# A batched fp32 matrix product on one core: engine programs written out by hand, a loop on TensorE, and loads with longer source runs

## The chip, the cores and the metric

The kernel runs on one core of a Trainium2 chip. A core has TensorE (PE in the profile, with its weight loads as PEld), VectorE (DVE), ScalarE (ACT), GpSimd (POOL) and SyncE (SP), which here issues every data transfer, and 16 DMA engines, which carry them out. The metric is the device time of one execution in microseconds; a figure for a kernel is the median of its runs.

## The reference

```python
def setup_inputs():
    batch, m, k, n = 16, 512, 768, 1024
    return {
        "x": np.random.randn(batch, k, m).astype(np.float32),
        "y": np.random.randn(batch, k, n).astype(np.float32),
    }

def reference(x: np.ndarray, y: np.ndarray) -> np.ndarray:
    return np.einsum('bkm,bkn->bmn', x, y).astype(np.float32)
```

For each of 16 batches a 768 x 512 matrix, transposed, is multiplied by a 768 x 1024 matrix. Inputs and output are fp32 in DRAM: 75.5 MB are read and 33.55 MB written.

## The kernel before

**Tiling.** K = 768 is split as 128 partitions times 6, with k = 6p + ko, so partition p of an x tile holds six consecutive rows of x, which are 12 KB in a row in DRAM, and partition p of a y tile holds 24 KB in a row. The output's 512 rows are split as 128 partitions times 4, m = 4p + mo, so that an output partition is 16 KB in a row. `x_w` (line 71) picks, for each `mo`, the 128 columns of x that belong to it.

**Stages of a batch b.** SP loads x (line 59) and y (line 62) into fp32 tiles `xs` and `ys`. DVE casts x to bf16 (line 67) and y in two halves of three ko each (line 70). PE runs 48 matmuls of 128 x 128 by 128 x 512 (line 83): for each `mo` of 4, for each half `nt` of N, six ko that add up in PSUM. After each `mo` ACT copies 1,024 columns of `ps` into `o_sb` (line 88). SP stores the whole 2 MB of `o_sb` (line 52), `LAG` = 4 batches later: in SP's order the store of batch b-4 follows the loads of batch b (lines 63 and 64), and the last four stores stand at the end (lines 89 and 90).

**Buffers.** Pools give two buffers each of `xs`, `ys`, `x_sb` and `y_sb`, five of `o_sb`, and four of `ps` with two PSUM banks each.

**Order and waits.** The program is written for one pass in order, `tc.manual_schedule()` keeps this order on each engine, and the tile framework derives the semaphore waits from the buffers. So the load of x of batch b waits for the cast of x of batch b-2 (which frees `xs`), and the load of y of batch b for the casts of y of batch b-2. The cast of x of batch b waits for the matmuls of batch b-2, which read the same `x_sb`. The engines' programs are unrolled: PE has 768 weight loads and 768 matmuls in a row.

**Last batch.** For b = 15 `halves` is 2: y is loaded in two transfers of three ko, and PE takes the first three ko of all output columns, then the other three, so that it can begin on half of y.

Of the kernel before, what the change touches and what calls it, by code (L numbers as in the profile page):

```python
# [1 line left out]

_os.environ.setdefault("NEURON_RT_ULTRASERVER_MODE", "4")

# [1 line left out]

# [4 lines left out]


@with_exitstack
def kernel(
    ctx: ExitStack,
    tc: tile.TileContext,
    x: bass.AP,
    y: bass.AP,
    out: bass.AP,
):  # L20
    nc = tc.nc
    P = 128
    FP32 = mybir.dt.float32
    BF16 = mybir.dt.bfloat16

    B, K, M = x.shape
    _, _, N = y.shape
    KT = K // P
    MT = M // P
    NF = 512  # L30
    NT = N // NF

    x_v = x.rearrange("b (p ko) m -> b p ko m", ko=KT)
    y_v = y.rearrange("b (p ko) n -> b p ko n", ko=KT)
    o_v = out.rearrange("b (p mo) n -> b p mo n", mo=MT)

    xs_pool = ctx.enter_context(tc.tile_pool(name="xs_pool", bufs=2))
    ys_pool = ctx.enter_context(tc.tile_pool(name="ys_pool", bufs=2))  # L40
    x_pool = ctx.enter_context(tc.tile_pool(name="x_pool", bufs=2))
    y_pool = ctx.enter_context(tc.tile_pool(name="y_pool", bufs=2))
    o_pool = ctx.enter_context(tc.tile_pool(name="o_pool", bufs=5))
    psum = ctx.enter_context(tc.tile_pool(name="psum", bufs=4, space=bass.MemoryType.PSUM))
    LAG = 4
    KH = KT // 2
    o_tiles = {}

    def store(b):
        o_sb = o_tiles.pop(b)  # L50

        nc.sync.dma_start(o_v[b], o_sb[:])

    with tc.manual_schedule():
        for b in range(B):
            xs = xs_pool.tile([P, KT, M], FP32, name="xs")
            ys = ys_pool.tile([P, KT, N], FP32, name="ys")
            halves = 2 if b == B - 1 else 1
            nc.sync.dma_start(xs[:], x_v[b])  # L59
            for h in range(halves):  # L60
                ks = slice(h * KT // halves, (h + 1) * KT // halves)
                nc.sync.dma_start(ys[:, ks], y_v[b, :, ks])
            if b >= LAG:
                store(b - LAG)
            x_sb = x_pool.tile([P, KT, M], BF16, name="x_sb")
            y_sb = y_pool.tile([P, KT, N], BF16, name="y_sb")
            nc.vector.tensor_copy(x_sb[:], xs[:])  # L67
            for h in range(2):
                ks = slice(h * KH, (h + 1) * KH)
                nc.vector.tensor_copy(y_sb[:, ks], ys[:, ks])  # L70
            x_w = x_sb[:].rearrange("p k (j mo) -> p k mo j", mo=MT)
            o_sb = o_pool.tile([P, MT, N], FP32, name="o_sb")
            o_tiles[b] = o_sb
            ps = {}


            for h in range(halves):
                for mo in range(MT):
                    if h == 0:
                        ps[mo] = psum.tile([P, NT, NF], FP32, name="ps")  # L80
                    for nt in range(NT):
                        for kt in range(h * KT // halves, (h + 1) * KT // halves):
                            nc.tensor.matmul(  # L83
                                ps[mo][:, nt], x_w[:, kt, mo],
                                y_sb[:, kt, nt * NF:(nt + 1) * NF],
                                start=(kt == 0), stop=(kt == KT - 1))
                    if h == halves - 1:
                        nc.scalar.copy(o_sb[:, mo].rearrange("p (t f) -> p t f", f=NF), ps[mo][:])  # L88
        for b in sorted(o_tiles):
            store(b)  # L90


# [1 line left out]
_INS = ['x', 'y']  # L94
_OUTS = [((16, 512, 1024), 'float32')]


# [23 lines left out]
```

## Time and profile before

| | us |
|---|---|
| median of 10 runs (261.58 to 262.20) | 262.01 |
| the profiled execution | 261.74 |
| its span, from the first instruction to the last | 260.0 |

| in the span | busy us | instructions |
|---|---|---|
| PE matmuls (line 83) | 186.3 | 768 |
| PE weight loads | 88.5 | 768 |
| DVE casts (lines 67 and 70) | 83.1 | 48 |
| ACT copies (line 88) | 64.9 | 64 |

PE, PEld, DVE and ACT work beside each other, so their busy times don't add up to the span. The profile cuts the span into 40 slices of 6.5 us. The DMA row of the slices gives, in tenths, the mean busy share of the 16 DMA engines; the row below it gives what they moved. The queue rows give the number of packets, the megabytes and the share of 16 engines' span: q1 is SP's queue of data transfers, and q8 and q14 carry instructions to the engines. Each transfer here makes 128 data packets, one for each partition, eight on each DMA engine, and 16 completion marks of 4 bytes, one from each engine. In the chain of waits each piece is followed back to what released it. In timeline lines the columns are start, duration, engine, line, operation and tiles, and in brackets the idle time before and what ended it.

The profile shows SP issuing the transfers in 0.3 to 0.4 us each. The median from issue to landing is 29.7 us for x, 28.1 us for y and 32.6 us for a store.

### The profile page before, as it was taken

To read this page: it belongs to the slowest core of one execution; us is meant where nothing else is said; L and a number is where in the kernel's file an instruction comes from. 1 tells how busy PE (TensorE), PEld (TensorE's weight loads), DVE (VectorE), ACT (ScalarE), POOL (GpSimd) and SP (SyncE) were. 2 spreads that over 40 slices of the span, in tenths; PEclk is the share of its full clock that TensorE was granted. 3 is DMA by queue.
4 is the path that set the end of the run, shared out by engine and by line. 5 is a ranking of instruction groups with operands and counts; after the bars stand their busy time and mean duration, and the time that the engine had idled before them with its cause. 6 is when DMAs were issued, how large, how long until landed. Compare 5 with 4: busy or idle time off the path is not lost.

```text
span 260.0 us, 1815 instructions
## 1 busy us (share of the span) xinstructions
PE 186.3 (72%) x768; PEld 88.5 (34%) x768; DVE 83.1 (32%) x48; ACT 66.2 (25%) x65; POOL 0.2 (0%) x4
## 2 busy tenths in 40 slices
PE   0049999898939949698594987939679394899600
PEld 0014555453513414243151442514334152355200
DVE  0271734525222252322524214252132522252000
ACT  1003343333321313314032140412314033131600
POOL 0000000000000000000000000000000000000000
PEclk9999999999986988979799797998999899799975
DMA  6999999999999999999999999999999999999995
GB/s 272 431 424 427 446 418 439 435 372 429 436 432 424 436 422 444 422 433 422 437 435 427 437 420 437 434 422 441 425 430 433 413 442 422 426 432 429 434 429 232
DMA packets 7065, 109.18 MB, mean 420 GB/s; under 512 B 784, under 2 KB 784, under 8 KB 784
## 3 DMA queue, kind: packets, MB, share of 16 engines
q1 hardware_dynamic: 7056, 109.06, 98.5%
q8 instruction: 6, 0.10, 0.1%
q14 instruction: 3, 0.02, 0.0%
HBM read 75.50 MB, written 33.55 MB: 419 GB/s over the span
## 4 chain that ended last, share of the span: by engine, by line
DMA 74%; DVE 11%; PE 8%; ACT 0%; issue 0%; SPq 0%; DVEq 0%
DMA ys<-in_y_dram 74%; DVE y_sb L70 11%; PE ps L83 8%; ACT o_sb L88 0%; SPq L59 0%; DVEq L70 0%
## 5 line engine op out<-in xcount | busy, mean ns | idle before, releaser
L83 PE MATMUL ps<-y_sb,x_sb 128*128 128x512 bf16 x768 | 186.3, 404 | 58.1 <-DVE y_sb L70 58.1
L83 PEld LDWEIGHTS <-x_sb 128*128 128x128 bf16 x768 | 88.5, 117 | 155.5 <-issue 39.6
L88 ACT COPY o_sb<-ps 128x1024 f32<-128x1024 f32 x64 | 64.9, 1014 | 178.6 <-PE ps L83 178.6
L70 DVE CAST y_sb<-ys 128x3072 bf16<-128x3072 f32 x32 | 54.9, 1756 | 87.7 <-DMA ys<-in_y_dram 87.7
L67 DVE CAST x_sb<-xs 128x3072 bf16<-128x3072 f32 x16 | 28.2, 1760 | 65.8 <-DMA xs<-in_x_dram 65.5
L88 ACT ACT_TABLE_LOAD x1 | 1.3, 1283 | 0.7 <-PEq L105 0.7
L105 POOL MEMSET const-bfloat16-1.0<- 128x1 bf16 x1 | 0.1, 101 | 0.0
L105 POOL MEMSET const-uint8-127<- 128x1 uint8 x1 | 0.1, 101 | 0.0
L105 POOL MEMSET const-float32-0.0<- 128x1 f32 x1 | 0.1, 98 | 0.2 <-issue 0.2
L105 POOL MEMSET const-float32-1.0<- 128x1 f32 x1 | 0.1, 98 | 0.0
## 6 DMA issues: line engine op xcount, KB each, us to landing
ys<-in_y_dram SPq DMA_DIRECT2D x15, 3072.0 KB, 28.1
out_dram<-o_sb SPq DMA_DIRECT2D x16, 2048.0 KB, 32.6
xs<-in_x_dram SPq DMA_DIRECT2D x16, 1536.0 KB, 29.7
ys<-in_y_dram SPq DMA_DIRECT2D x2, 1536.0 KB, 26.1
```

The lines of the kernel that those rows point to most:

```text
L67: nc.vector.tensor_copy(x_sb[:], xs[:])
L70: nc.vector.tensor_copy(y_sb[:, ks], ys[:, ks])
L83: nc.tensor.matmul(ps[mo][:, nt], x_w[:, kt, mo], y_sb[:, kt, nt * NF:(nt + 1) * NF], start=(kt == 0), stop=(kt == KT - 1))
L88: nc.scalar.copy(o_sb[:, mo].rearrange("p (t f) -> p t f", f=NF), ps[mo][:])
L105: nc = _bacc.Bacc("TRN2", target_bir_lowering=False, num_devices=1)
```

## The change

Instead of one program from which the framework derives the waits, each engine's program is written out with its own semaphores, inside a `tile_critical` region:

- **Semaphores.** `sx`, `sy` and `so` count finished transfers by buffer, `ready` counts casts that PE has not yet used, `room` counts free PSUM buffers, `groups` counts finished groups of 24 matmuls (two per batch), and `outs` counts finished output batches at the end.
- **PE** runs a loop of eight passes, each with two batches (`batch(0)`, `batch(1)`), so that the buffers' addresses are fixed. It takes credits: it waits for `ready` or `room` and subtracts what it took. [...] PE's list shrinks from 1,536 weight loads and matmuls to a body of 192 matmuls with their weight loads and a branch.
- **PSUM** is two buffers of four banks, one for each group (two `mo`), and ACT copies 2,048 columns at once: 32 copies in place of 64.
- **SP** loads x and y of batch b once the first group of batch b-2 is done (`groups` at 2(b-2)+1). The store of batch b waits for all groups of batch b+1, and for the last two batches for `outs`.
- **Wide loads.** `wide_dma` builds the first load of x and of y as before. From batch 1 on it makes the source access pattern of 32 rows of 48 KB for x (four partitions' worth) and of 64 rows of 48 KB for y (two partitions' worth); the destination stays 128 partitions of 12 KB or 24 KB.
- **Last batch.** y of batch 15 is loaded in one transfer, and PE goes through it like any other batch.
- At the end SP waits for each of the five `so`.

DVE's casts and their number, the matmuls, the bytes moved, the number of buffers in SBUF, and the order of the transfers on SP are the same, except for the split of the last y.

The launch code and the imports (`copy`, and `OrderedEngineSet`, which names the engines of a loop) are left out here.

```diff
@@ -36,58 +38,121 @@
     y_v = y.rearrange("b (p ko) n -> b p ko n", ko=KT)
     o_v = out.rearrange("b (p mo) n -> b p mo n", mo=MT)
 
-    xs_pool = ctx.enter_context(tc.tile_pool(name="xs_pool", bufs=2))
-    ys_pool = ctx.enter_context(tc.tile_pool(name="ys_pool", bufs=2))
-    x_pool = ctx.enter_context(tc.tile_pool(name="x_pool", bufs=2))
-    y_pool = ctx.enter_context(tc.tile_pool(name="y_pool", bufs=2))
-    o_pool = ctx.enter_context(tc.tile_pool(name="o_pool", bufs=5))
-    psum = ctx.enter_context(tc.tile_pool(name="psum", bufs=4, space=bass.MemoryType.PSUM))
     LAG = 4
+    NO = 5
     KH = KT // 2
-    o_tiles = {}
+
+    ctx.enter_context(tc.tile_critical())
+    ec = ctx.enter_context
+    xs = [ec(nc.sbuf_tensor(f"xs{i}", [P, KT, M], FP32)) for i in range(2)]
+    ys = [ec(nc.sbuf_tensor(f"ys{i}", [P, KT, N], FP32)) for i in range(2)]
+    xb = [ec(nc.sbuf_tensor(f"xb{i}", [P, KT, M], BF16)) for i in range(2)]
+    yb = [ec(nc.sbuf_tensor(f"yb{i}", [P, KT, N], BF16)) for i in range(2)]
+    ob = [ec(nc.sbuf_tensor(f"ob{i}", [P, MT, N], FP32)) for i in range(NO)]
+
+    HB = MT // 2
+    ps = [ec(nc.psum_tensor(f"ps{i}", [P, HB, NT, NF], FP32)) for i in range(2)]
+    sx = [ec(nc.semaphore(f"sx{i}")) for i in range(2)]
+    sy = [ec(nc.semaphore(f"sy{i}")) for i in range(2)]
+    so = [ec(nc.semaphore(f"so{i}")) for i in range(NO)]
+    ready = ec(nc.semaphore("ready"))
+    room = ec(nc.semaphore("room"))
+    groups = ec(nc.semaphore("groups"))
+    outs = ec(nc.semaphore("outs"))
+
+
+    made = {}
+
+    def wide_dma(key, dst, src, dram_rows, load):
+
+
+        if key not in made:
+            made[key] = nc.sync.dma_start(dst, src)
+            return made[key]
+        pat = mybir.BassSymbolicTensorAccessPattern
+        widen = lambda a: a.rearrange("(q r) k m -> q (r k m)", r=dram_rows)
+        plain = lambda a: a.rearrange("p k m -> p (k m)")
+        s, d = (widen(src), plain(dst)) if load else (plain(src), widen(dst))
+        return nc.sync.add_instruction(_copy.replace(
+            made[key].ins, name=nc.get_next_instruction_name(),
+            ins=(pat(ap=s.ap, dtype=s.dtype, bass_ap=s, is_dma=False),),
+            outs=(pat(ap=d.ap, dtype=d.dtype, bass_ap=d, is_dma=False),),
+            sync_info=None, ant_dge_precooked=False))
+
 
     def store(b):
-        o_sb = o_tiles.pop(b)
-
-        nc.sync.dma_start(o_v[b], o_sb[:])
-
-    with tc.manual_schedule():
-        for b in range(B):
-            xs = xs_pool.tile([P, KT, M], FP32, name="xs")
-            ys = ys_pool.tile([P, KT, N], FP32, name="ys")
-            halves = 2 if b == B - 1 else 1
-            nc.sync.dma_start(xs[:], x_v[b])
-            for h in range(halves):
-                ks = slice(h * KT // halves, (h + 1) * KT // halves)
-                nc.sync.dma_start(ys[:, ks], y_v[b, :, ks])
-            if b >= LAG:
-                store(b - LAG)
-            x_sb = x_pool.tile([P, KT, M], BF16, name="x_sb")
-            y_sb = y_pool.tile([P, KT, N], BF16, name="y_sb")
-            nc.vector.tensor_copy(x_sb[:], xs[:])
-            for h in range(2):
-                ks = slice(h * KH, (h + 1) * KH)
-                nc.vector.tensor_copy(y_sb[:, ks], ys[:, ks])
-            x_w = x_sb[:].rearrange("p k (j mo) -> p k mo j", mo=MT)
-            o_sb = o_pool.tile([P, MT, N], FP32, name="o_sb")
-            o_tiles[b] = o_sb
-            ps = {}
 
 
-            for h in range(halves):
-                for mo in range(MT):
-                    if h == 0:
-                        ps[mo] = psum.tile([P, NT, NF], FP32, name="ps")
-                    for nt in range(NT):
-                        for kt in range(h * KT // halves, (h + 1) * KT // halves):
-                            nc.tensor.matmul(
-                                ps[mo][:, nt], x_w[:, kt, mo],
-                                y_sb[:, kt, nt * NF:(nt + 1) * NF],
-                                start=(kt == 0), stop=(kt == KT - 1))
-                    if h == halves - 1:
-                        nc.scalar.copy(o_sb[:, mo].rearrange("p (t f) -> p t f", f=NF), ps[mo][:])
-        for b in sorted(o_tiles):
-            store(b)
+        if b < B - 2:
+            nc.sync.wait_ge(groups, 2 * (b + 2))
+        else:
+            nc.sync.wait_ge(outs, b - (B - 3))
+        nc.sync.dma_start(o_v[b], ob[b % NO][:]).then_inc(so[b % NO], 16)
+
+    for b in range(B):
+        i = b % 2
+        if b >= 2:
+
+            nc.sync.wait_ge(groups, 2 * (b - 2) + 1)
+        wide_dma("x", xs[i][:], x_v[b], 4, True).then_inc(sx[i], 16)
+        wide_dma("y", ys[i][:], y_v[b], 2, True).then_inc(sy[i], 16)
+        if b >= LAG:
+            store(b - LAG)
+    for b in range(B - LAG, B):
+        store(b)
+
+
+    for b in range(B):
+        i = b % 2
+        n = 16 * (b // 2 + 1)
+        if b >= 2:
+            nc.vector.wait_ge(groups, 2 * (b - 1))
+        nc.vector.wait_ge(sx[i], n)
+        nc.vector.tensor_copy(xb[i][:], xs[i][:]).then_inc(ready, 1)
+        nc.vector.wait_ge(sy[i], n)
+        for h in range(2):
+            ks = slice(h * KH, (h + 1) * KH)
+            nc.vector.tensor_copy(yb[i][:, ks], ys[i][:, ks]).then_inc(ready, 1)
+
+
+    def batch(i):
+        x_w = xb[i][:].rearrange("p k (j mo) -> p k mo j", mo=MT)
+        nc.tensor.wait_ge(ready, 2).then_inc(ready, -2)
+        for g in range(2):
+            nc.tensor.wait_ge(room, 1).then_inc(room, -1)
+            for m in range(HB):
+                for nt in range(NT):
+                    for kt in range(KT):
+                        if g == 0 and m == 0 and nt == 0 and kt == KH:
+                            nc.tensor.wait_ge(ready, 1).then_inc(ready, -1)
+                        mm = nc.tensor.matmul(
+                            ps[g][:, m, nt], x_w[:, kt, g * HB + m],
+                            yb[i][:, kt, nt * NF:(nt + 1) * NF],
+                            start=(kt == 0), stop=(kt == KT - 1))
+            mm.then_inc(groups, 1)
+
+    pe = nc.tensor.engine
+    with nc.Fori(0, B // 2, engines=OrderedEngineSet([pe]), head_slot={pe: 0}):
+        batch(0)
+        batch(1)
+
+
+    nc.scalar.nop().then_inc(room, 2)
+    for b in range(B):
+        if b >= NO:
+            nc.scalar.wait_ge(so[b % NO], 16 * (b // NO))
+        for g in range(2):
+            nc.scalar.wait_ge(groups, 2 * b + g + 1)
+            cp = nc.scalar.copy(ob[b % NO][:, g * HB:(g + 1) * HB].rearrange("p m (t f) -> p m t f", f=NF),
+                                ps[g][:])
+            if b < B - 1:
+                cp.then_inc(room, 1)
+        if b == B - 2:
+            nc.scalar.drain().then_inc(outs, 1)
+    cp.then_inc(outs, 1)
+
+    for i in range(NO):
+        nc.sync.wait_ge(so[i], 16 * len(range(i, B, NO)))
```

## The prediction

> **What bounds the kernel now.** I read the page first: busy shares, the slices, the DMA queues, the chain. Then the chain in order of time, the timeline of the first 25 us, the stages, and last the packet records behind the DMA rows.
>
> The page, queues and slices:
>
> ```profile
> span 260.0 us, 1815 instructions
> ...
> DMA  6999999999999999999999999999999999999995
> GB/s 272 431 424 427 446 418 439 435 372 429 436 432 424 436 422 444 422 433 422 437 435 427 437 420 437 434 422 441 425 430 433 413 442 422 426 432 429 434 429 232
> DMA packets 7065, 109.18 MB, mean 420 GB/s; under 512 B 784, under 2 KB 784, under 8 KB 784
> ...
> q1 hardware_dynamic: 7056, 109.06, 98.5%
> q8 instruction: 6, 0.10, 0.1%
> q14 instruction: 3, 0.02, 0.0%
> ```
>
> The 16 DMA engines are busy from slice 1 to the last one. No engine program has that: PE 72%, DVE 32%, ACT 25%. So work taken off PE, DVE or ACT is worth nothing by itself; only what starts the transfers sooner, makes them shorter, or evens them out over the 16 engines moves the end.
>
> The stages (span, PE, PEld, DVE, ACT, POOL, clock, DMA share, GB/s) say the same:
>
> ```profile
> 15.00:40.00 25.00, 23.29 (x98) 11.40 (x98) 13.32 (x8) 7.27 (x8) 0.00 (x0) 1.00 1.01 433
> ...
> 160.00:200.00 40.00, 31.91 (x137) 15.45 (x136) 12.13 (x7) 11.15 (x11) 0.00 (x0) 0.94 1.01 432
> ...
> 240.00:260.00 20.00, 4.42 (x21) 2.09 (x19) 0.00 (x0) 4.05 (x4) 0.00 (x0) 0.74 0.86 366
> ```
>
> A batch moves 6.8 MB, so at 430 GB/s it takes 15.85 us, and in the chain the loads of y follow each other by 31.7 us per two batches. The end of the chain:
>
> ```profile
> 190.93 28.08 DMA ys<-in_y_dram
> ...
> 219.10 3.44 DVE y_sb L70 x2
> 222.54 0.04 issue
> 222.59 21.84 PE ps L83 x93
> 244.43 0.02 issue
> 244.45 1.01 ACT o_sb L88
> ```
>
> It stops at 245.5 with the last copy, but the span ends at 260.0. The last store is issued at 245.5 and lands 13.6 us later, though its eight 16 KB packets per engine need only 8 x 0.61 = 4.9 us: it stands behind store 14. The tail is transfers too, with a good 8 us to spare for PE and ACT.
>
> The packet records refine it. Typical packets took 460 ns (12,288 B), 611 ns (16,384 B) and 912 ns (24,576 B); all of q1 together makes 255.9 us per engine. There is next to no idle left. What is left is unevenness: the 16 completion marks of one transfer lie 1.11 us apart for the first x and 2.80 us apart for the last store. Each 16 KB fetch on q8 (at 37.5, 68.2, 115.4, 153.3, 195.3 and 237.3 us, 0.9 to 1.1 us each) makes one engine late: at 115.36 a fetch took 1.01 us, and a y packet at 116.36 took 1.41 instead of 0.91. That is about 1.5 us for the engine hit, and nothing brings an engine back. After one fetch one mark lags, after six, six lag. The end is set by the latest engine.
>
> [...] the PE instructions on record before the six fetches number 175, 435, 707, 949, 1201 and 1473, about 256 apart. No loop is in this trace. [...] Here 12,288 B more cost 452 ns more, 27.2 GB/s per engine[...] Here successive 12,288 B packets of one engine start 457 ns apart, 5 ns over their 452 ns[...]
>
> **Part by part.** The sum is against the profiled execution: 261.74 us, which is its span of 260.0 and 1.74 around it. It lies 0.27 below the median of 262.01; I carry that difference over.
>
> *PE loop.* PE's 1,538 unrolled instructions become one loop of 192 matmuls, run eight times. With their weight loads that is 384 and a few control instructions: [...] the six fetches go. What is late next is the natural spread of 1.1 us, so the gain is 2.80 - 1.11 = 1.7. Three 8 KB fetches of other engines (191, 197 and 223 us, 0.31 us each) may stay; I take -1.5, between -1.7 and, with every pass fetching, +1.3 (rival B). A back edge that stalls PE is covered: PE waits 3 to 4 us for y_sb before each batch from batch 4 on ("3.30 <-DVE y_sb" at 220.9), and the edge is reached while earlier matmuls still run. Without that cover each of seven edges would cost what its stall has beyond those 3 us, first in PE's time, and in the end's only past the 8 us of the tail.
>
> *Load waits.* Before, x of batch b+2 is issued after the cast of x of batch b, y after the casts of y. Now both, and the store behind them in SP's order, wait for the first group (24 matmuls) of batch b. In steady state nothing comes of it: the group ends some 9 us after y of batch b has landed, and three more transfers and a store (4.9 + 3.7 + 7.3 + 4.9 = 20.8 us) are queued then. At the start it bites. Before, the issues were:
>
> ```profile
> 1.64 0.42 SPq L59 DMA_DIRECT2D xs<-in_x_dram  x1
> 2.10 0.84 SPq L62 DMA_DIRECT2D ys<-in_y_dram  x1
> ...
> 9.19 0.33 SPq L59 DMA_DIRECT2D xs<-in_x_dram  x1
> ...
> 18.12 0.33 SPq L62 DMA_DIRECT2D ys<-in_y_dram  x1
> ...
> 24.30 1.02 ACT L88 COPY o_sb<-ps 128x1024 f32<-128x1024 f32 x1 [1.58 <-PE ps L83]
> ```
>
> The second copy, at 24.30, shows when 24 matmuls are done: 24.2. That is the issue of x of batch 2, instead of 9.19. From issue to first packet the first transfer took 1.0 us (0.73 to 1.74), so the new data starts at 25.2, spread by 1.1. The first four loads end between 24.55 and 25.63. The engines thus stand still for 0.65 us if they restart in the order in which they ran dry, and the last one for up to 1.3 us if not. I take +0.8 (0.5 to 1.3). Batch 3's loads come at 34.5 + 1.0 against a queue that then lasts until 36.3, batch 4's at about 45 + 1 against 48: no second gap.
>
> *Wide loads.* From batch 1 on, x is read as 32 rows of 48 KB instead of 128 of 12 KB, y as 64 of 48 KB instead of 128 of 24 KB; the SBUF side keeps its rows. Per engine and batch 6 + 4 = 10 reads fewer; 15 batches x 10 x 5 ns = 0.75 us if the 5 ns sit on the read side, 0 if on the write side. No row here tells: -0.4 (-0.75 to 0).
>
> *Tail.* y of batch 15 is no longer split, PSUM goes out in 32 copies of 2,048 instead of 64 of 1,024. y lands by about 234, its first cast takes 1.76, 48 matmuls 10.5 to 12.5, the last copy about 2 x 1.0, issue and start 1.4: store 15 is ready at 249 to 251.5; the first engines finish store 14 at 251.5. Zero, and what is lost at worst hits engines that are ahead. Stores 12 to 14 wait for a later batch's groups or for ACT, and come over 7 us before their turn.
>
> *Start and end.* A further hop between SP and the other engines at the start, and five completion waits at the end. The whole start barrier shows before as one wait of 0.7 us (ACT on PE's sequencer): I take a part of that for the hop and the end together, +0.2 (0 to 0.6). The added drain and the credits sit on ACT and PE, inside their idle time.
>
> Sum: -1.5 + 0.8 - 0.4 + 0.2 = -0.9; 260.8 for the profiled execution, 261.1 as a median.
>
> **Rivals.**
>
> *B, the loop is fetched anew.* For it: [...] nothing in the trace excludes it. [...] At 1.5 us for the engine hit, 16 put one on every engine, and the end is 1.5 + 1.1 against 2.8 before: a gain of only 0.2. Above 16, some engine is hit twice, 3.0 + 1.1: 1.3 later than before. With the other terms (+0.6) that is 261.74 + 1.9, about 263.9 as a median. It ends slower from about 16 fetches on; at 6 to 8 it is +0.6.
>
> *C, the wide loads change which engine writes which partitions.* [...] The place is every load from batch 1 on. [...] It decides as soon as packets of loads take longer than 460 or 912 ns by over 1%. For it: nothing but the missing row. [...]
>
> *D, gain and gap cancel.* The fetches stop, but the restart at 25 us takes the whole 1.3 and the read side gives nothing, with 0.6 for start and end: 262.0 to 262.5. For it: the sum's terms are all of one size.
>
> **How the numbers follow.** The forecast A has 0.55, B 0.22, C 0.08, D 0.15. A measurement of this kernel tells about 0.2% (0.5 us) from no change. A alone lies between 260.1 (all terms at their best: -1.7 + 0.5 - 0.75 = -1.95 from the median) and 262.0; 0.3 for the spread of the runs goes below it. Faster: A 0.41, B 0.03, D 0.02, in all 0.46. Same: A 0.13, B 0.06, D 0.06: 0.25. Slower: A 0.01, B 0.13, C 0.08, D 0.07: 0.29. The range reaches up to B's price and leaves C out: 259.8 to 263.9.
>
> **What would show it.** In the changed kernel's page: q8 with no more than two packets (A) or 16 and more (B); the marks of the last store within about 1.3 us; a dent in the GB/s row at 25 us; load packets at their old time per byte (against C); the last copy before 249. Wrong would be an end that moves without the q8 row moving, or a gap beyond the first 30 us.

## The result: 1.9% slower, and the profile after

The changed kernel takes 266.93 us (median of 9 runs, 265.86 to 268.0) against 261.95 us before (30 runs): a ratio of 1.0193, interval 1.0182 to 1.0204. The prediction had 261.1 us and a range up to 263.9. The profiled execution took 265.57 us, with a span of 263.6; it is the fastest of its kind, so its profile shows a loss of 3.8 us (265.57 against 261.74), where the medians differ by 5.0.

The page of the changed kernel, span, DMA slices and queues:

```profile
span 263.6 us, 1831 instructions
...
DMA  7996999997989999899999989999899999989995
GB/s 258 434 466 276 418 418 418 380 455 301 495 370 447 470 420 442 378 470 415 470 395 415 485 368 442 470 418 452 383 457 420 465 395 418 475 372 433 433 420 234
...
q1 hardware_dynamic: 4512, 109.05, 97.6%
q8 instruction: 1, 0.02, 0.0%
q14 instruction: 1, 0.01, 0.0%
```

The engines still carry the time: 97.6% of the span on q1. The instruction fetches did go, from six on q8 to one. Packets fell from 7,056 to 4,512, since a 48 KB source row now counts as one. The dent is in the fourth slice (19.8 to 26.4 us): DMA at 6 tenths, 276 GB/s.

The stage (span, PE, PEld, DVE, ACT, POOL, clock, DMA share, GB/s) from 24 to 28 us in the kernel before:

```profile
24.00:28.00 4.00, 4.00 (x21) 2.05 (x19) 2.34 (x2) 2.03 (x2) 0.00 (x0) 1.00 1.02 436
```

and that stage with two later ones in the changed kernel:

```profile
24.00:28.00 4.00, 4.00 (x21) 2.09 (x19) 0.95 (x1) 1.87 (x1) 0.00 (x0) 1.00 0.61 209
...
34.00:38.00 4.00, 4.00 (x20) 2.14 (x19) 0.00 (x0) 1.87 (x1) 0.00 (x0) 1.00 0.91 393
...
46.00:50.00 4.00, 4.00 (x21) 2.06 (x19) 0.00 (x0) 1.87 (x1) 0.00 (x0) 1.00 0.97 406
```

SP's timeline of the changed kernel, its fifth to tenth transfer:

```profile
25.33 0.47 SPq L70 DMA_DIRECT2D xs<-in_x_dram  x1
25.85 0.59 SPq L70 DMA_DIRECT2D ys<-in_y_dram  x1
35.69 0.47 SPq L70 DMA_DIRECT2D xs<-in_x_dram  x1
36.21 0.59 SPq L70 DMA_DIRECT2D ys<-in_y_dram  x1
47.58 0.47 SPq L70 DMA_DIRECT2D xs<-in_x_dram  x1
48.09 0.59 SPq L70 DMA_DIRECT2D ys<-in_y_dram  x1
```

Before, the load of x of batch 2 was issued at 9.19 us; here at 25.33, while the first DMA engine had finished all four first loads at 24.81 and the last at 27.02. (Such times are those of the completion marks of a transfer: it has landed when the last of its 16 marks is there. VectorE's cast of the first x, for one, starts at 8.78 us, after marks from 6.51 to 8.75.) The loads of batches 2, 3 and 4 are 10 to 12 us apart, which is TensorE's time for one batch. TensorE's own timeline says why: it is dense there.

```profile
23.63 17.21 PE L128 MATMUL ps<-yb,xb 128*128 128x512 bf16 x79
```

The end of the chain in order of time:

```profile
241.78 10.72 PE ps L128 x45
252.50 0.02 issue
252.52 1.86 ACT ob L146
```

As before it stops at the last copy, now 254.4 us. Store 14 ends on the first engine at 255.33 and on the last at 257.61; store 15 follows at once and ends on the last at 262.43. So no time was lost at the tail itself. Nearly all of it lies ahead of batch 5: y of that batch has landed at 79.92 us instead of 76.31, and from then on a batch takes 15.83 us, against 15.85 before.

### The profile page after: what moved, and what is told of

Its sections match the earlier page's. It is cut to its first block, busy times and chain, and to the rows that moved or that the text cites. A ratio compares the mean times of both kernels' runs of the same rounds, so it can differ in the third digit from the quotient of the medians.

```text
span 263.6 us, 1831 instructions
## 1 busy us (share of the span) xinstructions
PE 186.3 (71%) x768; PEld 86.7 (33%) x768; DVE 83.0 (31%) x48; ACT 61.1 (23%) x33; POOL 0.2 (0%) x4
## 3 DMA queue, kind: packets, MB, share of 16 engines
q1 hardware_dynamic: 4512, 109.05, 97.6%
## 5 line engine op out<-in xcount | busy, mean ns | idle before, releaser
L128 PE MATMUL ps<-yb,xb 128*128 128x512 bf16 x768 | 186.3, 403 | 66.2 <-PEq L122 59.2
L128 PEld LDWEIGHTS ps<-yb,xb 128*128 128x128 bf16 x768 | 86.7, 116 | 165.3 <-issue 99.4
L146 ACT COPY ob<-ps 128x2048 f32<-128x2048 f32 x32 | 59.8, 1869 | 192.3 <-PE ps L128 192.3
L115 DVE CAST yb<-ys 128x3072 bf16<-128x3072 f32 x32 | 54.9, 1756 | 88.8 <-DMA ys<-in_y_dram 88.8
L111 DVE CAST xb<-xs 128x3072 bf16<-128x3072 f32 x16 | 28.2, 1760 | 69.8 <-DMA xs<-in_x_dram 69.8
```

The lines of the kernel that those rows point to most:

```text
L111: nc.vector.tensor_copy(xb[i][:], xs[i][:]).then_inc(ready, 1)
L115: nc.vector.tensor_copy(yb[i][:, ks], ys[i][:, ks]).then_inc(ready, 1)
L128: mm = nc.tensor.matmul(ps[g][:, m, nt], x_w[:, kt, g * HB + m], yb[i][:, kt, nt * NF:(nt + 1) * NF], start=(kt == 0), stop=(kt == KT - 1))
L146: cp = nc.scalar.copy(ob[b % NO][:, g * HB:(g + 1) * HB].rearrange("p m (t f) -> p m t f", f=NF), ps[g][:])
```

## The experiments

Each kernel is the changed one with the edit shown; the ratio is to the kernel before, whose median was 262.1 to 262.2 us in these comparisons. Two theories led: **L**, the late issue of loads costs the time, and **W**, the wide reads do.

### Early waits

The load of x of batch b waits for the cast of x of batch b-2, and y for the casts of y, as before the change.

```diff
+    cast = ec(nc.semaphore("cast"))
-            nc.sync.wait_ge(groups, 2 * (b - 2) + 1)
+            nc.sync.wait_ge(cast, 2 * (b - 2) + 1)
         wide_dma("x", xs[i][:], x_v[b], 4, True).then_inc(sx[i], 16)
+        if b >= 2:
+            nc.sync.wait_ge(cast, 2 * (b - 2) + 2)
...
         nc.vector.tensor_copy(xb[i][:], xs[i][:]).then_inc(ready, 1)
+        nc.vector.drain().then_inc(cast, 1)
...
             nc.vector.tensor_copy(yb[i][:, ks], ys[i][:, ks]).then_inc(ready, 1)
+        nc.vector.drain().then_inc(cast, 1)
```

> The changed kernel (266.93 us), but the loads of batch b wait, as in the kernel before, for the casts of batch b-2 (a new semaphore, raised by VectorE after the x cast and after the y casts) and not for TensorE's first group. Theory L (the late issue makes the gap at 25 us, and each late restart brings slow packets after it): x of batch 2 is issued near 10 us, the slices show no dent at 25 us, and the time falls by 2 to 3 us, to 264 to 265. Theory W (the wide reads are slow when the queue is short): slow packets stay at 38 and 50 us and the time stays above 265.5. Theory S (the start is slower by itself, 1.4 us at the landing of the first x): the first x still lands at 8.7 us rather than 7.4.

Measured: 262.86 us, ratio 1.0031 (1.0021 to 1.0041). That is 4.07 us less than the changed kernel, more than L itself had expected. The first issues in SP's timeline, and the first two of the same stages:

```profile
10.76 0.47 SPq L71 DMA_DIRECT2D xs<-in_x_dram  x1
19.73 0.47 SPq L71 DMA_DIRECT2D ys<-in_y_dram  x1
21.75 0.47 SPq L71 DMA_DIRECT2D xs<-in_x_dram  x1
30.72 0.47 SPq L71 DMA_DIRECT2D ys<-in_y_dram  x1
```

```profile
24.00:28.00 4.00, 4.00 (x20) 2.13 (x19) 0.78 (x1) 1.87 (x1) 0.00 (x0) 1.00 0.92 393
...
34.00:38.00 4.00, 4.00 (x21) 2.05 (x20) 0.00 (x0) 1.53 (x1) 0.00 (x0) 1.00 1.04 442
```

The stage at 24 us goes from 0.61 to 0.92 busy. TensorE does the same work in it (4.00 us busy in both), which is why only the DMA column tells the two apart. The share counts a packet where it starts, so with 48 KB packets a full stage can read under or over 1 (0.92 and 1.04 above).

The packet records add the size. Idle time is meant per engine, and "slow" is the time by which packets took over 0.05 us more than is usual for their size, also per engine:

```
                         changed kernel   early waits
idle, 24 to 28 us             2.05            0
idle, 36 to 40 us             0.21            0
slow, 24 to 30 us             0.58            0
slow, 34 to 42 us             0.37            0
slow, 48 to 54 us             0.47            0
slow, 54 to 62 us             1.13            0.56
```

The differences add up to 4.2 us per engine. The idle time is half of it. The other half is slow packets: up to 2.7 us instead of 1.82 after the restart and at the start of the next two loads, which were issued only 2 to 3 us ahead of their turn, and up to 2.97 us in y of batch 4 (2.61 with early waits). The sum is close to the 4.07 us between the medians, but it doesn't prove them, for these two executions differ by only 2.34 us (265.57 and 263.23). With early waits the engines lose time later on: store 15 is issued at 252.20 us, after the first engine has finished store 14 (251.45), and they stand still there for 1.1 us each. The latest engine doesn't wait, but it is further behind the others (the marks of store 14 are 3.72 us apart, 2.28 in the changed kernel), and it sets the end. So the table shows where the time goes, and its split is no more than rough. L holds, W falls here already; S holds as well, since the first x still lands at 8.90 us.

### Plain loads, with late and with early waits

```diff
-        if key not in made:
+        if True:
```

> The changed kernel with every load built as the first one is (128 rows on both sides); the late waits stay. Theory L: the gap at 25 us stays and the time is within 1 us of the changed kernel, 266 to 268. Theory W: the slow packets after 25 us go and the time falls to 263 to 265. If the wide reads save what the packets suggest (1,824 against 4 x 457 ns), the steady batch takes 0.02 us more than with them.

> Both edits at once: early waits and plain loads, so that the PE loop, the two PSUM buffers and the hand-written waits remain. Theory L: as the run with early waits alone, within 0.5 us. Theory W: better than that one by 1 us and more. If the saved instruction fetches are worth 1.5 us at the end, as the prediction had it, this run is below the kernel before: 260.5 to 261.5; if the start is slower by itself, it is 262 to 263.

Measured: plain loads with late waits 266.49 us (1.0177, 1.0146 to 1.0208, so not told apart from the changed kernel); with early waits 263.04 us (1.0031, 1.0020 to 1.0043) against 262.86 with wide loads. The idle stretch at 25 us (2.2 us) and the slow packets after it are there with plain loads too. So the wide reads are not to blame, and they bring about 0.2 us at most: most packets of 49,152 bytes took 1,815 or 1,829 ns, against 4 x 457 = 1,828 ns or 2 x 909 = 1,818. The last theory of this expectation, a saving of 1.5 us from the fetches, fell.

### The loop written out again, with early waits

```diff
-    with nc.Fori(0, B // 2, engines=OrderedEngineSet([pe]), head_slot={pe: 0}):
+    for _ in range(B // 2):
         batch(0)
         batch(1)
```

> Early waits and wide loads, but TensorE's loop written out as eight passes in a row[...]. If fetches matter as the prediction had it: six or more 16 KB fetches come back, the completion marks of the last store spread over 2.5 us and more, and the time is 1 to 1.7 us above the run with early waits alone. If the spread of the marks comes from the start and not from fetches: within 0.5 us of it.

The page has the six fetches back:

```profile
q8 instruction: 6, 0.10, 0.1%
```

Measured: 262.76 us, 1.0021 (1.0013 to 1.0029), the same as the loop's 262.86. The marks of store 14 lie 3.68 us apart here and 3.72 us with the loop. In the loop kernel one engine falls behind at once: there is a jump to the placed head (`head_slot`) at 1.14 us and one fetch of 931 ns at 4.27 us, in the middle of the first load. The marks of the first x are 2.35 us apart with it and 1.08 without, and the first x has landed at 8.90 us and 7.55: most of what S saw is this fetch.

It delays TensorE's start too. All eight kernels with the placed head have such a fetch (at 4.1 to 4.6 us), and their first y has landed at 16.03 to 16.49 us; in the four without it (this one and the next three) it has at 14.71 to 15.04. VectorE's cast of it, in the changed kernel and in the first of the next three:

```profile
16.08 3.43 DVE L115 CAST yb<-ys 128x3072 bf16<-128x3072 f32 x2 [5.54 <-DMA ys<-in_y_dram]
```

```profile
14.74 3.43 DVE L119 CAST yb<-ys 128x3072 bf16<-128x3072 f32 x2 [5.53 <-DMA ys<-in_y_dram]
```

### Loop kernels with the fetch elsewhere, and with none

Three edits on top of the early waits. The first drops the placed head, and the other two keep that and add one edit each:

```diff
-    with nc.Fori(0, B // 2, engines=OrderedEngineSet([pe]), head_slot={pe: 0}):
+    with nc.Fori(0, B // 2, engines=OrderedEngineSet([pe])):
```

> The run with early waits[...]. Theory F (the jump to a fresh block brings a 16 KB fetch at 4.3 us that makes one engine 1.3 us late in the first x load, so one fetch costs the end as much as six did): no 16 KB fetch at 4 us, the marks of the first x within 1.2 us instead of 2.35, and, [...] 261.6 to 262.2. If the body now [...] is fetched anew in each pass: ten or more 16 KB fetches and 263 to 264.5. If the 2.35 us have another cause: unchanged, 262.6 to 263.1.

Measured: 262.86 us, 1.0025 (1.0014 to 1.0036). The fetch moved to 37.9 us. The marks of the first x are 0.89 us apart, as theory F had it, but with the fetch they go from 0.88 to 2.26 (x of batch 3), and the time stays: F's time fell.

The second puts ko outside and N's halves inside:

```diff
-                for nt in range(NT):
-                    for kt in range(KT):
-                        if g == 0 and m == 0 and nt == 0 and kt == KH:
-                            nc.tensor.wait_ge(ready, 1).then_inc(ready, -1)
+                for kt in range(KT):
+                    if g == 0 and m == 0 and kt == KH:
+                        nc.tensor.wait_ge(ready, 1).then_inc(ready, -1)
+                    for nt in range(NT):
```

> Early waits, no placed loop head, and in TensorE's body ko outside and the two halves of N inside, so that two successive matmuls use the same weights. If the weight load is then issued once for both, the body shrinks from 202 to about 154 instructions [...]. Theory F (a single fetch in the loop kernels makes one engine 1.3 us late, and the end follows the latest engine): no 16 KB fetch at all, marks of the last store before the last within 2.3 us instead of 3.5, 261.3 to 262.0. If the loads of weights stay or a fetch remains: 262.6 to 263.1.

Measured: 262.77 us, 1.0023 (1.0014 to 1.0033). All 768 weight loads stayed, so the body did not shrink, and one fetch came at 38.3 us: this run could not test what it was made for. The third leaves out half of the sum over K instead:

```diff
-                    for kt in range(KT):
-                        if g == 0 and m == 0 and nt == 0 and kt == KH:
+                    for kt in range(KH):
+                        if g == 1 and m == 0 and nt == 0 and kt == 0:
...
-                            start=(kt == 0), stop=(kt == KT - 1))
+                            start=(kt == 0), stop=(kt == KH - 1))
```

> Early waits, no placed loop head, and TensorE adds up only the first three of the six ko: half of the sum over K is left out, everything else (casts, transfers, copies) stays. The body has about 106 instructions. Theory F: no 16 KB fetch, the marks 1.3 us closer together at the end than in the run without a placed head, and 261.2 to 261.9. If the fetch did not set the end, 262.6 to 263.1 although TensorE does half of its work.

Now q8 is gone from the queue rows of the page:

```profile
q1 hardware_dynamic: 4512, 109.05, 98.3%
q14 instruction: 1, 0.01, 0.0%
```

Measured: 262.70 us, 1.0023 (1.0015 to 1.0030). The marks stay within 0.9 us up to 85 us, but then grow without any fetch by TensorE, in steps, each with a cluster of slow y packets (at 88, 96 and 216 us, for example), to 2.66 us at the end. So none, one or six fetches end alike, at 262.70, 262.86 and 262.76 us: the latest engine is late either way. Theory F is refuted as to the time, as long as the waits are early.

### How far the late wait reaches

The waits of single batches were moved, with the condition in place of `...` being `b == 2`, `b > 2`, `b in (2, 3)` or `b in (2, 3, 4)` for the early ones. Where it holds, y has its own wait for the casts as in the run with early waits:

```diff
-            nc.sync.wait_ge(groups, 2 * (b - 2) + 1)
+            if ...:
+                nc.sync.wait_ge(cast, 2 * (b - 2) + 1)
+            else:
+                nc.sync.wait_ge(groups, 2 * (b - 2) + 1)
```

> The changed kernel, but the loads of batch 2 alone wait for the casts; those of batches 3 to 15 keep the late wait. Theory R (every restart with little lead costs: the gap at 25 us cost 2.6 us of the 4.1, the slow packets at 38, 49 and 58 us the rest, because those loads were issued only 2 to 3 us ahead of their turn): the dent at 25 us goes, slow packets stay near 37 and 48 us, and the time is about 264.3, half way between the changed kernel (266.9) and the run with early waits (262.9). Theory G (one gap, whose disorder causes the slow packets later): 262.9 to 263.3, and no slow packets before 54 us.

> The reverse: only the loads of batch 2 keep the late wait for TensorE's first group, batches 3 to 15 wait for the casts. Theory R: a gap at 25 us worth 2.6 us, then no slow packets at 38 and 50 us: about 265.4. Theory G: the gap brings the slow packets with it: 266.5 to 267.

Only batch 2 late: 265.55 us (1.0127, 1.0110 to 1.0144), as theory R said. One gap with its restart costs 2.7 us, and the slow packets at 38 and 50 us are gone with the late waits of batches 3 and 4. Only batch 2 early: 265.80 us (1.0125, 1.0095 to 1.0156), not the 264.3 expected. The stage shows that the gap did not go but moved:

```profile
34.00:38.00 4.00, 4.00 (x20) 2.10 (x19) 0.00 (x0) 1.87 (x1) 0.00 (x0) 1.00 0.83 283
```

Neither R nor G had this. x of batch 3 is issued at 35.97 us, when the first engine has just finished y of batch 2 (the marks come from 35.82 to 38.10). The engines stand still for 1.64 us each. The new theory was P, that TensorE paces the late loads until it has caught up.

> The changed kernel, but the loads of batches 2 and 3 wait for the casts and those of batches 4 to 15 keep the late wait. With batch 2 alone the gap did not go but moved from 25 to 36 us. Theory P (TensorE, dense until batch 4, paces the late loads, so the gap moves on to the next late load until TensorE has caught up): the gap moves to 47 to 50 us, shorter now, and the time is 263.6 to 264.6. Theory Q (the shift in that run was chance, and one early batch more ends it): 262.9 to 263.3, no idle engines between 30 and 60 us.

265.66 us (1.0131, 1.0110 to 1.0153), above P's figure, but the gap is where P put it (1.64 us idle per engine again; 2.05 in the changed kernel):

```profile
46.00:50.00 4.00, 4.00 (x20) 2.15 (x19) 0.93 (x1) 1.87 (x1) 0.00 (x0) 1.00 0.63 209
```

> The changed kernel, but the loads of batches 2, 3 and 4 wait for the casts and those of batches 5 to 15 keep the late wait. Theory P (TensorE paces the late loads only until it has caught up with the transfers, near 60 us): batch 5's loads are then issued near 57 us, with y of batch 4 and a store still queued, no engine stands still between 30 and 250 us, and the time is that of the run with early waits throughout, 262.6 to 263.1: the late wait is free from batch 5 on. If the gap moves on once more: an idle stretch near 58 to 65 us and 264 to 265.7.

262.85 us (1.0034, 1.0018 to 1.0050): with three batches early the gap is gone, and the late wait from batch 5 on is free. P holds on where the gap goes and where it ends; that it shrinks on the way, it had wrong. With batch 2 late alone, with batches 3 and on, or with batches 4 and on, there is one gap of 1.6 to 1.9 us, at the first late load, and the time is 2.7 to 2.9 us above that with early waits throughout.

## Why the prediction was wrong, point by point

**What bounds the kernel** was right: every difference above is one of the DMA engines' time, and with early waits halving TensorE's work moved nothing that can be measured (262.70 against 262.86 us).

**Load waits** is the step that failed. It put the late issue at +0.8 us (0.5 to 1.3); the runs put it at 4.1. It saw the gap at 25 us, but mis-sized it three times. It took the start of the gap from a y that landed at 14.65 us; in the changed kernel it landed at 16.05, so the issue came at 25.33 and not at 24.2. It counted only idle time, and that as 0.65 to 1.3 where 2.05 was measured, and nothing for the packets after a restart, though the kernel before showed such packets at its start (up to 1.21 us instead of 0.46). And its sentence "no second gap" was right on idle time (0.21 us) but not on cost: the loads of batches 3 and 4 came 2 to 3 us ahead of their turn, and began with slow packets.

The late landing of the first y comes for the most part from another term of the sum, the loop with its fetch in the first load. How much of the gap that makes is open, since no run has late waits without this fetch. The end of the first group shifts less than the landing, because TensorE's first matmuls follow each other 0.43 us apart and only later ones 0.21 (from 21.7 us on in the changed kernel, from 22.5 in the one with early waits and no placed head). ACT's first copy, which follows that group, comes at 24.18, 24.80 and 25.14 us in the three kernels without the fetch that do all the work, and at 25.34 in the changed kernel. By these figures the gap would be 0.2 to 1.2 us shorter without the fetch: an estimate, not shown.

Why the late wait costs only at the start is what the runs with single batches show. Until batch 5, loads take about 11 us per batch and TensorE's batches 10 to 12 us, so loads tied to TensorE gain hardly any lead. After that a store is added to each batch, transfers take 15.8 us, and the wait is free, as predicted.

**PE loop.** The fetches went, from six to one, as forecast A said. That a loop would end them was the author's estimate: the runs show the counts (six with the loop written out, one or none with it) and not the cause. Rival B did not occur, and the back edges cost nothing that shows: in the changed kernel the first is on record at 36.92 us (222 ns), while the matmuls of its pass run on to 40.84, and with early waits the loop takes 262.86 us against 262.76 written out. But the term of -1.5 us was worth nothing (262.70 to 262.86 us for none, one and six fetches, with early waits). Its premise was that nothing but fetches makes one engine late. The run without any fetch shows that slow packets do it as well (marks up to 2.66 us apart), and in the kernels with a placed head the single fetch falls into the first load and takes 1.3 us of an engine there. Nor does a late engine stay late in every case: the standstill at 25 us brought it back (marks 2.21 us apart for y of batch 1, ahead of the gap, and 0.86 for x of batch 2, after it). The text also had the body wrong, here and in the change's description: it is 96 matmuls with 96 weight loads, 202 instructions with the credits and the branch in the trace, and not 384. The kernels that jump to the placed head have a fetch 3 us later (in the changed kernel the jump is at 1.13 us, and the fetch takes 931 ns from 4.12 us), those without the jump have none there, and the changed kernel's seven back edges brought none. A stall is not to be seen, since TensorE waits for the first casts until 17.88 us.

**Wide loads**: -0.4 predicted (-0.75 to 0), about -0.2 measured with early waits, inside the runs' spread, and +0.4 with late waits (266.93 against 266.49), not told apart from 0 either. Rival C, for whose cause no trace had anything, is excluded: 49,152 bytes in 1,815 to 1,829 ns are 27 GB/s per engine, as 24,576 bytes in 912 ns were. No saving by longer reads is seen in these packet times; the writes kept their 128 rows, and on which side the 5 ns sit stays open.

**Tail**: 0 predicted, 0 measured.

**Start and end**: +0.2 predicted (0 to 0.6), about 0.7 in the profiles: the first packet at 1.97 us and not 1.74, 1.58 us from the last packet to the end of the span and not 1.24, and 1.92 us around the span of 263.65 and not 1.77 around 259.97. The last of these the prediction did not have. It agrees with what the kernels with early waits and wide loads still lose to the one before, 0.6 to 0.75 us; that nothing else goes into this rest is not shown.

The sum of -0.9 us was 5.9 off: 3.3 of this are the load waits, 1.5 the loop, 0.5 start and end and 0.2 the wide loads. With the measured terms the sum is 0 + 4.1 - 0.2 + 0.7 = 4.6 against 4.98 measured. Of what is missing, 0.2 us is that the kernel before took 262.14 us beside the early waits and 261.95 beside the changed kernel. None of the variants was faster than the kernel before; those with early waits up to batch 4 at least are 0.2% to 0.3% slower.

## What to carry to other kernels

When DMA engines bound a kernel, a wait that is moved to a later event must be checked against the filling of the pipeline, where the lead is smallest, and not only in steady state; and it must be priced with what follows a restart, not with the idle time alone. Where several transfers are tied to the same slow event, freeing one of them moves the gap to the next (here from 25 us to 36 and then to 47). A load has landed when its latest engine is done, so one engine held up in it (by 1.3 us here) delays all that waits for it. A cause of unevenness among engines is worth removing only if it is the one that makes the latest engine late: here six fetches, one and none gave 262.76, 262.86 and 262.70 us.

## What was not expected of the hardware

- After a standstill the first packets are slow: up to 1.8 us instead of 0.46 (12,288 bytes) at the start of the changed kernel, up to 2.5 us instead of 1.82 (49,152 bytes) after its gap, and up to 3.1 us where batch 2 alone was late. Loads of x issued 2 to 3 us ahead of their turn began in the same way with next to no standstill; x of batch 5, issued 3.6 us ahead (batch 2 alone early) or 7.7 us (changed kernel), did not. What makes them slow stayed open.
- Packets of y of batch 4, just ahead of the first store's, were slow in every kernel: 0.5 to 0.8 us per engine in the kernel before and those with early waits, 1.0 to 1.3 us in the kernels with a gap at 25 or 47 us. Why was not tried.
- The runs of the changed kernel lie up to 2.4 us apart (265.57 to 268.0), the 30 of the kernel before 0.6. TensorE's slow start, which now times loads and does not end at the same time in each profile, would be one reason; it was not tried.
